# Score products of a differential-attention head in program order: the two maps take turns on the two halves of the TensorE array

## The chip, the cores and the metric

The kernel runs on one core of a Trainium2 chip. The metric is device time in microseconds (us) of one execution; lower is better.

## What is computed

The reference is one encoder block on 1024 tokens of width 1024, all in float32: an adaLN modulation, one input projection for two groups of heads, their attention, an output projection, a SwiGLU feed-forward part and a last RMSNorm. The change is in the products of queries and keys. Group A (8 heads of 64 channels) attends within a window of the grid; group B is differential attention, 4 heads with two softmax maps each:

```python
s = jnp.einsum('bhmqd,bhmkd->bhmqk', qb, kh).astype(jnp.float32)
s = s - slopes[:, None, None, None] * dist
p = jax.nn.softmax(s, axis=-1)
a = p[:, :, 0] - lam * p[:, :, 1]
return jnp.einsum('bhqk,bhke->bhqe', a.astype(vh.dtype), vh)
```

Here `m` counts the two maps of a head, each with 64 channels of its own for q and k.

## The kernel before

Every float32 product is made of three products of rounded parts: a value is split into a high part (type fp32r) and the rest, and high by high, low by high and high by low are summed in PSUM. So each score takes three matmuls.

The work runs in stages: modulation and the norm of x; the input projection and group A (class `Na`, PSUM tiles `ns`); group B (class `Da`, tiles `s`), which the trace shows from 305.7 to 607.2 us; the output projection; the feed-forward part (tiles `gu` and `dn`). Group B goes by units: one head h and 128 query rows i, 32 units in all. In this text unit "0_3" is head 0, i = 3.

A unit of group B does this:

- `Da.score` takes two PSUM tiles `s{h}_{i}_{m}` of 128x1024 from the pool `big`, which has two buffers; so map m of the next unit needs the buffer that map m of this one gives back. `scores` writes 12 matmuls for it, 6 for each map: two halves of 512 keys by three part products. Map 0 has its q and k in partitions 0 to 63, map 1 in 64 to 127 (`r = slice(64 * m, 64 * m + 64)`), and so each stands on its own half of the rows of the array. In the text of the program the maps alternate matmul by matmul.
- VectorE (DVE) reads each map out of PSUM (L686: adds the distances, takes the minimum), which frees the buffer; ScalarE (ACT) takes the exponent (L688).
- `Da.trans`: DVE combines the two maps (L701), TensorE transposes the result (tiles `at`), ACT copies it out of PSUM (`ath`, L708) and DVE makes the low part (`atl`, L709).
- `Da.pv`, after every second unit: 24 products with v (tiles `pv`).

Between these steps the list `seq` lets `fill` put in products of other stages as fillers: projections of the next heads (`q`, `k`, `v1p`), and for head 3 the output projection (`mo`). Their results leave the four PSUM buffers of the pool `bank` by ACT and DVE too (L460 and L461 for q, L468 and L469 for k). `next(mods)` puts in one step of the modulation on DVE (L602, `acc`).

What order an engine runs is set when the program is built: the tile framework schedules with its own timeline of costs, and keeps the order that it comes to. The class `InOrder` can hold instructions to the program's order by an edge (`after`) that costs no semaphore. On TensorE (`PE`) such edges are used for the first stage (`PE.chain`) and switched off before the heads; so in group B the scheduler chooses.

Of the kernel before, what the change touches and what calls it, by code (L numbers as in the profile page):

```python
# [104 lines left out]
def block_kernel(ctx: ExitStack, tc: tile.TileContext, t: dict):  # L105
    nc = tc.nc
    V, A, G, PE, SY = nc.vector, nc.scalar, nc.gpsimd, InOrder(tc, nc.tensor), nc.sync
# [74 lines left out]
    def rstd_of(ssq, name):  # L182
        r = sm.tile([P, 2], F32, tag="rstd", bufs=6, name=name)
        G.tensor_scalar(out=r[:, 0:1], in0=ssq, scalar1=1.0 / D, scalar2=EPS, op0=ALU.mult, op1=ALU.add)
        G.tensor_tensor(out=r[:, 1:2], in0=r[:, 0:1], in1=mhalf[:, 0:1], op=ALU.pow)
        return r[:, 1:2]
# [189 lines left out]
    for n in range(4):  # L376
        for j in range(4):
            PE.matmul(pms[0][:, 4 + n:5 + n], wada_t[0][j][:, n * P:(n + 1) * P], silc[:, j:j + 1],
                      start=j == 0, stop=j == 3)
# [263 lines left out]

    def scores(dsts, q, k, qsl, ksl):

        for ti, (z, w) in enumerate([(0, 0), (1, 0), (0, 1)]):
            for m in range(2):
                r = slice(64 * m, 64 * m + 64)
                PE.matmul(dsts[m], q[z][r, qsl], k[w][r, ksl], start=ti == 0, stop=ti == 2)

    def p_t(name):
        return mp.tile([P, S], F32, tag="p", bufs=4, name=name)
# [8 lines left out]
    class Da:  # L661
# [3 lines left out]
        def score(self):  # L665
            h, i = self.h, self.i
            if i == 0:
                need(("q", h)), need(("k", h))
                if h:
                    V.tensor_scalar(out=dists[0], in0=dists[0], scalar1=0.25, scalar2=None, op0=ALU.mult)  # L670
                else:
                    tp.close()
                    dp = mx.enter_context(tc.tile_pool(name="dp", bufs=1, reuse_waits="tile"))
                    dists.append(dp.tile([P, 1920], F16, name="dist"))
                    SY.dma_start(out=dists[0], in_=t["dist"])
            q, k = qkv["q", h], qkv["k", h]
            self.st = sm.tile([P, 8], F32, tag="st", bufs=12, name=f"st{h}_{i}")
            self.p = []
            ss = [big(f"s{h}_{i}_{m}") for m in range(2)]
            for n in range(2):  # L680
                nsl = slice(n * 512, (n + 1) * 512)
                scores([s[:, nsl] for s in ss], q, k, slice(i * P, (i + 1) * P), nsl)
            for m, s in enumerate(ss):
                pr = p_t(f"p{h}_{i}_{m}")
                d0 = (56 - 8 * i) * 16
                V.tensor_tensor_reduce(out=pr, in0=s, in1=dists[0][:, d0:d0 + 1024], scale=1.0, scalar=BIG,  # L686
                                       op0=ALU.add, op1=ALU.min, accum_out=self.st[:, m:m + 1])
                A.activation(out=pr, in_=pr, func=AF.Exp, scale=-1.0, bias=self.st[:, m:m + 1],  # L688
                             accum_out=self.st[:, 2 + m:3 + m])
                self.p.append(pr)  # L690
# [78 lines left out]
    class Na:  # L769
# [3 lines left out]
        def score(self):  # L773
            pr, i = self.pr, self.i
            if i == 0:
                need(("nq", pr)), need(("nk", pr)), tables(pr)
            q, k, tb = qkv["nq", pr], qkv["nk", pr], qkv["tb", pr]
            j0, j1 = max(i - 1, 0), min(i + 1, 7)
            self.nk, self.j0 = (j1 - j0 + 1) * P, j0
            nk = self.nk  # L780
            d0 = 384 if i == 0 else (640 if i == 7 else 0)
            s = big(f"ns{pr}_{i}")
            self.st = st = sm.tile([P, 8], F32, tag="st", bufs=12, name=f"nst{pr}_{i}")
            self.p = p = mp.tile([P, 2, 384], F32, tag="p", bufs=4, name=f"np{pr}_{i}")
            scores([s[:, m * 512:m * 512 + nk] for m in range(2)], q, k,
                   slice(i * P, (i + 1) * P), slice(j0 * P, j0 * P + nk))
            for m in range(2):
                V.tensor_tensor_reduce(out=p[:, m, 0:nk], in0=s[:, m * 512:m * 512 + nk],
                                       in1=tb[m][:, d0:d0 + nk], scale=1.0, scalar=BIG,
                                       op0=ALU.add, op1=ALU.min, accum_out=st[:, m:m + 1])  # L790
                A.activation(out=p[:, m, 0:nk], in_=p[:, m, 0:nk], func=AF.Exp, scale=-1.0,
                             bias=st[:, m:m + 1], accum_out=st[:, 2 + m:3 + m])
# [346 lines left out]
    for gi, fs in enumerate(groups):  # L1139
# [42 lines left out]
        for i in range(NT):  # L1182
            isl = slice((i % 4) * P, (i % 4 + 1) * P)
            last = gi == len(groups) - 1
# [14 lines left out]
            if last:  # L1199
                V.tensor_tensor(out=ssq[:, 0:1], in0=ssq[:, 0:1], in1=ssq[:, 1:2], op=ALU.add)  # L1200
                r = rstd_of(ssq[:, 0:1], f"r3_{i}")
# [55 lines left out]
```

## Time and profile before

| | |
|---|---|
| median of 3 runs | 1409.25 us (1408.97 to 1409.38) |
| the profiled execution | 1409.35 us |
| its span, first to last instruction | 1407.6 us |
| mean granted TensorE clock | 0.985 |
| TensorE (PE) busy | 1370.6 us, 97% |
| VectorE (DVE) busy | 719.6 us, 51% |
| ScalarE (ACT) busy | 461.0 us, 33% |

The time of the execution is 1.75 us more than its span. Matmuls are pipelined: a row of the timeline gives the start of the first one, the time from there to the end of the last, and how many were merged; the end of a matmul is modelled, and the next can start before it. So the pace of matmuls is read from starts, and a group's length from a merged row. `x12` in a row of tile `s` is 12 matmuls without another tile between them; both maps have the same name there, since buffer numbers are left out.

### The profile page before, as it was taken

Reading aid. Unit: us, or ns where it says so; the run is one execution under the profiler, and the core shown is the slowest. Engines: PE = TensorE matmul, PEld = TensorE weight load, DVE = VectorE, ACT = ScalarE, POOL = GpSimd, SP = SyncE. Lnnn points to the kernel's source line nnn. Section 1 sums busy time; section 2 is a strip of 40 time slices with the busy share of each in tenths; the row PEclk is TensorE's granted clock in tenths of the full one; section 3 lists DMA queues with packets and bytes.
Section 4 is the critical chain, followed back from the end, with each engine's and each line's share of the span. In section 5 each row is a group of like instructions: output and inputs, shape, how many; then the busy total and the mean of one; then the engine's idle time right before and its main releaser. Section 6 shows DMA issues by size and latency. Waiting matters only on the chain.

```text
span 1407.6 us, 17672 instructions
## 1 busy us (share of the span) xinstructions
PE 1370.6 (97%) x7033; PEld 1136.7 (81%) x7033; DVE 719.6 (51%) x1324; ACT 461.0 (33%) x817; POOL 290.3 (21%) x318
## 2 busy tenths in 40 slices
PE   6899999999999999999999999999999999999997
PEld 5698888887887778878888888888888888888886
DVE  5765678768767688757837125113411421251136
ACT  5554544545443454434521110211121021202212
POOL 3012332321121100002422221221221031204201
PEclk7999999999999999999999999999999999999999
DMA  9222523431221251022331120210111121103102
GB/s 370 111 75 78 170 91 117 173 127 45 68 84 59 91 202 38 8 84 97 120 105 35 56 60 7 84 60 30 56 55 40 31 75 45 60 1 90 45 27 93
DMA packets 43826, 114.82 MB, mean 82 GB/s; under 512 B 12723, under 2 KB 12979, under 8 KB 42464
## 3 DMA queue, kind: packets, MB, share of 16 engines
q1 hardware_dynamic: 39280, 99.37, 20.9%
q0 software_dynamic: 4464, 14.33, 3.2%
q8 instruction: 55, 0.90, 0.3%
q14 instruction: 27, 0.22, 0.0%
HBM read 99.26 MB, written 14.42 MB: 81 GB/s over the span
## 4 chain that ended last, share of the span: by engine, by line
PE 91%; DVE 3%; ACT 2%; DMA 2%; issue 1%; POOL 1%; SPq 0%; DVEq 0%; POOLq 0%; ACTq 0%
PE gu L89 33%; PE dn L89 17%; PE s L89 5%; PE pv L89 3%; PE mo L89 3%; PE q L89 3%; PE k L89 3%; PE nk L89 2%; PE mp L89 2%; PE npv L89 2%; PE at L89 2%; PE v1p L89 2%; PE v0p L89 2%; PE v3p L89 2%; PE v2p L89 2%; PE nq L89 2%
## 5 line engine op out<-in xcount | busy, mean ns | idle before, releaser
L1164 DVE TENSOR_TENSOR sg<-sg,gu 128x512 f32<-128x512 f32 x44 | 30.2, 687 | 352.6 <-ACT sg L1163 352.6
L89 PE MATMUL dn<-wd_h,al 128*128 128x512 f32 x352 | 136.9, 389 | 0.0
L89 PE MATMUL dn<-wd_l,ah 128*128 128x512 f32 x352 | 136.9, 389 | 0.0
L89 PE MATMUL dn<-wd_h,ah 128*128 128x512 f32 x352 | 136.9, 389 | 0.0
L1194 DVE TENSOR_TENSOR dt<-dn,gate_f 128x512 f32<-128x512 f32 x96 | 66.4, 691 | 88.1 <-PE dn L89 88.1
L202 POOL TENSOR_TENSOR wg_l<-wg_r,wg_h 128x1024 fp32r<-128x1024 f32 x20 | 48.3, 2417 | 271.9 <-ACT wg_h L201 271.9
L201 ACT ACTIVATE wg_h<-wg_r 128x1024 fp32r<-128x1024 f32 x22 | 23.3, 1060 | 211.9 <-PE dn L89 154.2
L688 ACT ACTIVATE p<-p,st 128x1024 f32<-128x1024 f32 x64 | 73.4, 1148 | 58.8 <-DVE st L686 57.9
L686 DVE CUSTOM_DVE_ANT_0 p<-s,dist 128x1024 f32<-128x1024 f32 x64 | 76.7, 1220 | 19.2 <-PE s L89 18.4
L89 PE MATMUL s<-qk 64*128 64x512 f32 x384 | 82.5, 415 | 1.5 <-DVE st L686 1.5
L202 POOL TENSOR_TENSOR wd_l<-wd_r,wd_h 128x1024 fp32r<-128x1024 f32 x20 | 48.0, 2399 | 163.7 <-ACT wd_h L201 163.7
L89 PEld LDWEIGHTS dn<-wd_h,al 128*128 128x128 f32 x352 | 66.1, 188 | 13.7
L89 PEld LDWEIGHTS dn<-wd_h,ah 128*128 128x128 f32 x352 | 66.1, 188 | 13.7
L89 PEld LDWEIGHTS dn<-wd_l,ah 128*128 128x128 f32 x352 | 66.1, 188 | 13.7
L1163 ACT ACTIVATE sg<-gu 128x512 f32<-128x512 f32 x44 | 26.0, 590 | 138.9 <-PE gu L89 136.6
L1195 DVE TENSOR_TENSOR x<-x,dt 128x512 f32<-128x512 f32 x96 | 70.0, 729 | 2.9
L89 PEld LDWEIGHTS s<-qk 64*128 64x128 f32 x384 | 50.9, 184 | 22.7 <-issue 8.1
L89 PE MATMUL gu<-h2h,wg_h 128*128 128x512 f32 x176 | 68.9, 392 | 0.2 <-DVE sg L1164 0.2
L591 POOL DMA_DIRECT2D wm<-in_w_ada_l_dram x48 | 27.4, 570 | 202.2 <-DVE acc L602 100.7
L89 PE MATMUL gu<-h2l,wg_h 128*128 128x512 f32 x176 | 68.7, 391 | 0.0
L89 PE MATMUL gu<-h2h,wu_h 128*128 128x512 f32 x176 | 68.6, 390 | 0.0
L89 PE MATMUL gu<-h2l,wu_h 128*128 128x512 f32 x176 | 68.6, 390 | 0.0
(308 smaller groups left out, 3500.1 us busy)
## 6 DMA issues: line engine op xcount, KB each, us to landing
w_r<-in_w_in_dram SPq DMA_DIRECT2D x24, 512.0 KB, 3.9
wm<-in_w_ada_l_dram POOLq DMA_DIRECT2D x48, 256.0 KB, 3.0
wg_r<-in_w_gate_up_dram SPq DMA_DIRECT2D x22, 512.0 KB, 3.5
wu_r<-in_w_gate_up_dram SPq DMA_DIRECT2D x22, 512.0 KB, 3.5
wd_r<-in_w_down_dram SPq DMA_DIRECT2D x22, 512.0 KB, 3.5
x<-in_x_dram SPq DMA_DIRECT2D x16, 512.0 KB, 8.5
wada<-in_w_ada_s_dram SPq DMA_DIRECT2D x6, 1024.0 KB, 12.1
v<-vd SPq DMA_DIRECT2D x4, 1024.0 KB, 5.7
```

The source lines that it names most:

```text
L89: ins = call(*args, **kw)
L201: A.activation(out=hi, in_=raw, func=AF.Copy)
L202: lo_engine().tensor_tensor(out=lo, in0=raw, in1=hi.bitcast(F32), op=ALU.subtract)
L591: queue.dma_start(out=raws[-1], in_=t["w_ada_l"][which - 2, n, :, j, :])
L686: V.tensor_tensor_reduce(out=pr, in0=s, in1=dists[0][:, d0:d0 + 1024], scale=1.0, scalar=BIG, op0=ALU.add, op1=ALU.min, accum_out=self.st[ ...
L688: A.activation(out=pr, in_=pr, func=AF.Exp, scale=-1.0, bias=self.st[:, m:m + 1], accum_out=self.st[:, 2 + m:3 + m])
L1163: A.activation(out=sg, in_=gu[:, 0:512], func=AF.Silu)
L1164: V.tensor_tensor(out=sg, in0=sg, in1=gu[:, 512:1024], op=ALU.mult)
L1194: V.tensor_tensor(out=dt_, in0=out, in1=gtf[:, dsl], op=ALU.mult)
L1195: V.tensor_tensor(out=x1[i][:, dsl], in0=x1[i][:, dsl], in1=dt_, op=ALU.add)
```

## The change

Each matmul of a call of `scores` gets an edge to the one before it, so that the alternation of the maps that the program's text has is kept. Nothing is added to or left out of what is computed, and the number of TensorE instructions in the program is the same.

```diff
     def scores(dsts, q, k, qsl, ksl):
 
+        last = None
         for ti, (z, w) in enumerate([(0, 0), (1, 0), (0, 1)]):
             for m in range(2):
                 r = slice(64 * m, 64 * m + 64)
-                PE.matmul(dsts[m], q[z][r, qsl], k[w][r, ksl], start=ti == 0, stop=ti == 2)
+                mm = PE.matmul(dsts[m], q[z][r, qsl], k[w][r, ksl], start=ti == 0, stop=ti == 2)
+                if last is not None:
+                    PE.after(mm, last)
+                last = mm
```

The TensorE order is the same up to unit 0_0; group A's scores alternate in both kernels. In group B, before, most units have all of map 0 and then all of map 1. TensorE at unit 0_1, before (`q1` is a projection for head 1, the names end in numbers of the buffers):

```order
L89 MATMUL q1_0_3262<-hh3_165,w16_l_3257 128x512
L89 MATMUL s0_1_0_3303<-qk0_2951 128x512 x6
L89 MATMUL s0_1_1_3304<-qk0_2951 128x512 x6
L89 MATMUL at0_0_0_3367<-ident_79,p0_0_0_3287 128x128 x4
L89 MATMUL at0_0_1_3374<-ident_79,p0_0_0_3287 128x128 x4
```

The same place now; of the 12 rows of the unit the last four stand here:

```order
L89 MATMUL s0_1_0_3303<-qk0_2951 128x512
L89 MATMUL s0_1_1_3304<-qk0_2951 128x512
L89 MATMUL s0_1_0_3303<-qk0_2951 128x512
L89 MATMUL s0_1_1_3304<-qk0_2951 128x512
L89 MATMUL at0_0_0_3367<-ident_79,p0_0_0_3287 128x128 x4
L89 MATMUL at0_0_1_3374<-ident_79,p0_0_0_3287 128x128 x4
```

Where six of one map stood ahead of six of the other, the maps now alternate to the end. The transposes of unit 0_0 follow at once in both orders.

TensorE at unit 0_3, before:

```order
L89 MATMUL at0_1_0_3426<-ident_79,p0_1_0_3317 128x128 x4
L89 MATMUL at0_1_1_3433<-ident_79,p0_1_0_3317 128x128 x4
L89 MATMUL s0_3_0_3447<-qk0_2951 128x512 x6
L89 MATMUL s0_3_1_3448<-qk0_2951 128x512 x6
L89 MATMUL pv0_0_3473<-ath0_0_0_3360,v0_0_3344 128x256
L89 MATMUL s0_4_0_3540<-qk0_2951 128x512 x6
L89 MATMUL pv0_0_3473<-atl0_0_0_3362,v0_0_3344 128x256
```

And now:

```order
L89 MATMUL at0_1_0_3426<-ident_79,p0_1_0_3317 128x128 x4
L89 MATMUL at0_1_1_3433<-ident_79,p0_1_0_3317 128x128 x4
L89 MATMUL s0_3_0_3447<-qk0_2951 128x512
L89 MATMUL pv0_0_3473<-ath0_0_0_3360,v0_0_3344 128x256
L89 MATMUL s0_3_1_3448<-qk0_2951 128x512
L89 MATMUL s0_3_0_3447<-qk0_2951 128x512
L89 MATMUL s0_3_1_3448<-qk0_2951 128x512
```

One matmul of map 0 now stands alone, with one filler behind it, and then the other 11; map 0 can no longer be finished before map 1's buffer is free. Map 0 of unit 0_4 has left this place: it came one matmul behind unit 0_3, and now it comes after all 24 products `pv0_0`, the transposes of unit 0_2 and nine products of a projection.

DVE around the read of unit 1_7, before (L461 takes the low part of the projection `q2` out of PSUM, ISA at L686 is the read of a map):

```order
L701 SCALAR_TENSOR_TENSOR p1_6_0_4505<-p1_6_1_4508,st1_6_4490,p1_6_0_4505 128x1024
L709 TENSOR_TENSOR atl1_2_1_4463<-at1_4_1_4474,ath1_2_1_4461 128x4x128
L602 SCALAR_TENSOR_TENSOR acc41_4132<-wm414_4263,silc_89,acc41_4132 128x512
L686 ISA p1_7_0_4593,st1_7_4578<-s1_7_0_4579,dist_3270 128x1024
L686 ISA st1_7_4578 128x1
L461 SCALAR_TENSOR_TENSOR qk2_4353<-q2_1_4453,qk2_4353 128x512
```

And now (the lines have moved by four):

```order
L461 SCALAR_TENSOR_TENSOR qk2_4353<-q2_1_4453,qk2_4353 128x512
L702 RECIPROCAL st1_6_4490<-st1_6_4490 128x1
L703 SCALAR_TENSOR_TENSOR st1_6_4490<-st1_6_4490,lam_620 128x1
L705 SCALAR_TENSOR_TENSOR p1_6_0_4505<-p1_6_1_4508,st1_6_4490,p1_6_0_4505 128x1024
L713 TENSOR_TENSOR atl1_2_0_4462<-at1_5_0_4544,ath1_2_0_4460 128x4x128
L690 ISA p1_7_0_4593,st1_7_4578<-s1_7_0_4579,dist_3270 128x1024
```

The read of `q2_1` was behind the combination of unit 1_6 and the first read of unit 1_7, and is now ahead of both. On TensorE the products `k2_0` followed unit 1_7's scores by 12 small products; now those small products come ahead of the scores, and `k2_0` right behind.

## Rows read from the trace of the kernel before

**Rows 1.** The page, parts 1 and 4: busy time of each engine, and the chain by engine.
```profile
PE 1370.6 (97%) x7033; PEld 1136.7 (81%) x7033; DVE 719.6 (51%) x1324; ACT 461.0 (33%) x817; POOL 290.3 (21%) x318
...
PE 91%; DVE 3%; ACT 2%; DMA 2%; issue 1%; POOL 1%; SPq 0%; DVEq 0%; POOLq 0%; ACTq 0%
```

**Rows 2.** Windows of head 0 and group B: busy PE, PEld, DVE, ACT, POOL, clock, DMA.
```profile
305.70:362.80 57.10, 56.72 (x299) 43.02 (x298) 44.01 (x89) 28.26 (x51) 7.05 (x11) 1.00 0.20 70
...
305.70:607.20 301.50, 297.24 (x1705) 236.82 (x1705) 223.40 (x418) 139.83 (x236) 31.03 (x32) 0.98 0.22 77
```

**Rows 3.** The page, part 5, group B's scores: busy us, mean ns, idle before.
```profile
L89 PE MATMUL s<-qk 64*128 64x512 f32 x384 | 82.5, 415 | 1.5 <-DVE st L686 1.5
...
L89 PEld LDWEIGHTS s<-qk 64*128 64x128 f32 x384 | 50.9, 184 | 22.7 <-issue 8.1
```

**Rows 4.** Timeline of PE: start us, length us, engine, line, tiles, count.
```profile
312.52 2.24 PE L89 MATMUL s<-qk 64*128 64x512 f32 x12
...
335.01 0.40 PE L89 MATMUL k<-hh,w_h 128*128 128x512 f32 x1
...
335.24 0.39 PE L89 MATMUL k<-hl,w_h 128*128 128x512 f32 x1
...
368.68 0.50 PE L89 MATMUL s<-qk 64*128 64x512 f32 x1
...
377.06 1.65 PE L89 MATMUL s<-qk 64*128 64x512 f32 x6
...
389.89 0.28 PE L89 MATMUL v1p<-w_h,hl 128*128 128x256 f32 x1
390.01 0.28 PE L89 MATMUL v1p<-w_l,hh 128*128 128x256 f32 x1
390.22 1.65 PE L89 MATMUL s<-qk 64*128 64x512 f32 x12
```

**Rows 5.** Timeline of all engines, from unit 0_0's first read to its transposes.
```profile
308.54 1.23 DVE L686 CUSTOM_DVE_ANT_0 p<-s,dist 128x1024 f32<-128x1024 f32 x1 [4.22 <-PE s L89]
...
313.24 1.29 DVE L701 SCALAR_TENSOR_TENSOR p<-p,st,p 128x1024 f32<-128x1024 f32 x1
...
314.69 1.09 PE L89 MATMUL at<-ident,p 128*128 128x128 f32 x8
```

**Rows 6.** Timeline of DVE: the two reads of unit 1_2.
```profile
391.91 1.23 DVE L686 CUSTOM_DVE_ANT_0 p<-s,dist 128x1024 f32<-128x1024 f32 x1 [1.18 <-PE s L89]
...
393.06 1.22 DVE L686 CUSTOM_DVE_ANT_0 p<-s,dist 128x1024 f32<-128x1024 f32 x1
```

**Rows 7.** Groups of DVE in 305.7 to 607.2: busy, mean ns, idle before and releasers.
```profile
L686 DVE CUSTOM_DVE_ANT_0 p<-s,dist 128x1024 f32<-128x1024 f32 x62 | 74.4, 1220 | 19.1 <-PE s L89 18.4 <-PE at L89 0.4
L709 DVE TENSOR_TENSOR atl<-at,ath 128x512 fp32r<-128x512 f32 x60 | 40.3, 685 | 23.0 <-ACT ath L708 23.0
```

**Rows 8.** Timeline at 441 us: DVE's read of q2_1, and PE behind it.
```profile
440.99 0.68 DVE L461 SCALAR_TENSOR_TENSOR qk<-q,qk 128x512 fp32r<-128x512 f32 x1
...
441.72 0.79 PE L89 MATMUL k<-hh,w_h 128*128 128x512 f32 x1 [2.31 <-DVE qk L461]
442.31 0.63 PE L89 MATMUL k<-hl,w_h 128*128 128x512 f32 x1
442.74 0.63 PE L89 MATMUL k<-hh,w_l 128*128 128x512 f32 x1
```

**Rows 9.** Windows with a low clock (columns as in rows 2, the clock behind POOL).
```profile
441.00:448.00 7.00, 6.28 (x15) 4.94 (x16) 6.96 (x18) 2.48 (x4) 1.04 (x1) 0.51 0.25 99
...
516.00:519.60 3.60, 3.60 (x16) 3.23 (x15) 3.60 (x9) 1.99 (x5) 0.00 (x0) 0.53 1.03 421
```

**Rows 10.** Timeline at units 2_5 and 2_6: the last scores, the first read, the next scores.
```profile
508.23 1.43 PE L89 MATMUL s<-qk 64*128 64x512 f32 x10
...
513.30 1.22 DVE L686 CUSTOM_DVE_ANT_0 p<-s,dist 128x1024 f32<-128x1024 f32 x1
...
514.59 1.67 PE L89 MATMUL s<-qk 64*128 64x512 f32 x6 [1.08 <-DVE st L686]
```

## The prediction

> **What bounds the kernel now.** I read the busy time by engine first. TensorE is busy 97% of the span and is 91% of the chain that ended last [rows 1], so a TensorE stretch that gets shorter shortens the kernel, as long as nobody else is late. Then I cut out group B, the only place where the order changes. In its 301.5 us TensorE is busy 297.2 and VectorE 223.4; in head 0, which has the fewest fillers, VectorE is busy 44.0 of 57.1 us, 77% [rows 2]. So the stage is TensorE's, with VectorE a quarter behind.
>
> Next comes what the scores take there. Their 384 matmuls have TensorE busy for 82.5 us, with only 1.5 us of idle time before them [rows 3]. The timeline then says what an order is worth [rows 4]. At 377.06 six matmuls of one map take 1.65 us. At 390.22 twelve matmuls, which happen to alternate there, also take 1.65 us. At 312.52 twelve that go six by six take 2.24 us. So two matmuls on the two halves of the array run in the time of one, and before the change this happens in few places: by the order, 66 of the 192 matmuls of map 1 stand right behind one of map 0. In the changed order it is 178.
>
> **The change part by part.** *Scores.* Counted in the order of the changed kernel, they stand in 54 pieces. 23 are long: 16 with all 12 matmuls alternating, and 7 with 11, the first of map 0 having gone ahead; at 1.65 us [rows 4] they make 38.0. Ten are a single matmul of map 0; one takes 0.50 us [rows 4], together 5.0. The other 21 pieces hold 57 steps of a pair (or one left over). A further pair costs (1.65 - 0.50) / 5 = 0.23 us, which is also the distance of two full 512-column matmuls, 335.01 to 335.24 [rows 4]. So they take 21 x 0.50 + 36 x 0.23 = 18.8. The sum is 61.8 against 82.5 [rows 3]: **-20.7 us**.
>
> One mechanism could spoil that step: a half's next weights might have to wait until its matmul is done. A load of weights takes 184 ns [rows 3], so a step would be 0.184 + 0.23 = 0.41 us, where the row at 390.22 shows 0.23 for each pair. The Trainium skill, "TensorE: Matmul & The Clock Gate", Part 3, says that a weight load overlaps matmuls in flight only when its row group differs, which would make that wait the rule for alternating pairs too. By it the sum would be 23 x (0.50 + 5 x 0.41) + 5.0 + 21 x 0.50 + 36 x 0.41 = 89.0, so 6.5 us more than now. The measured row disagrees with it, and the sum goes by the row.
>
> *The edges* cost nothing by themselves: they order instructions of one engine and no semaphore is added.
>
> *New waits.* Until now map 0 of the next unit could start when map 0 of this unit had been read. Now the twelve are tied together, so they need both buffers. Both maps also finish together; the two reads then end at 393.06 + 1.22 = 394.28, 2.4 us after the scores that ended at 390.22 + 1.65 [rows 4, 6]. Where TensorE has less than that to do in between, it stands still, and the fillers, transposes and products with v behind it in its queue with it. I priced what stands between two units in the changed order by rows 4 (0.23 for 512 columns, 0.12 for 256, as 389.89 to 390.01) and row 314.69 for eight transposes [rows 5]. Of 31 gaps three are below 2.4: units 0_2 to 0_3 (1.5 us with the lone matmul: wait 0.9), 2_3 to 2_4 (1.5: 1.0) and 0_4 to 0_5 (2.3: 0.1). From 0_5 to 0_6 there are 2.9 us, but VectorE does two `atl` of 0.69 us [rows 7] and two like them between the pairs of reads; I take 1.3. After unit 0_0 the transposes wait for L701. That ends at 314.53 and they start at 314.69, just in time [rows 5]; as TensorE gets there 0.59 (2.24 - 1.65) and two 0.12 fillers earlier, it waits 0.8. At unit 2_6 VectorE is late: unit 2_5's scores end at 509.66, its first read starts at 513.30, and TensorE waits 1.08 for it [rows 10]. For the second read it would wait 1.2 to 1.7 longer if VectorE stays that late, and not at all if not: 0.8. The sum is **+4.9**, between 1.9 (the three gaps alone) and twice that.
>
> *Waits that go.* At 441.72 the projection `k2_0` waits 2.31 us for VectorE's L461, which starts at 440.99 [rows 8]. In the new order L461 is ahead of a combination of 1.29 us [rows 5] and a read of 1.22, and `k2_0` comes a piece of 1.65 us later: the wait goes. With it goes the low clock behind it. TensorE is at 0.51 of its clock (its level of 1.2 GHz) for 7.0 us [rows 9], matmuls start 0.43 apart instead of 0.23 [rows 4, 8], and half of the 7 us is lost. Unit 0_4's wait, 1.5 - 1.08 = 0.4 [rows 3, 10], goes too, since its scores have moved behind 24 products. **-2.3 - 3.4 - 0.4 = -6.1**; nothing at worst, if another collision comes in their place.
>
> *Clock.* A new wait can lower the clock again. Behind the waits at 510 to 516 it was at 0.53 for 3.6 us [rows 9], which loses 1.7. I take one such stretch, **+1.7**, with 0 and four of them, 6.8, as ends.
>
> *Other queues.* POOL has the memset that opens head 2's q buffer behind one more weight split, SP has a weight load and an x load on the other side of a neighbour. Each is needed only after tens of products of other tiles, which hide it; without that cover the memset would cost a split, some 2.4 us.
>
> The terms make -20.7 + 4.9 - 6.1 + 1.7 = -20.2. VectorE sets a limit a little below that. It idles 18.4 us waiting for scores [rows 7], and 223.4 us of work and its other waits, above all 23.0 for ScalarE [rows 7], stay, so the stage can hardly shrink by more than 18.4. I take **-18.4**. The profiled execution took 1409.35 us, 0.1 more than the median of the runs, so the forecast is **1391.0 us**; by itself it may be 1386 to 1396.
>
> **The rivals.** *VectorE takes half of it back.* With alternating maps its first read cannot start before nearly all twelve matmuls are done, whereas it used to read map 0 while TensorE made map 1. If only half of the 18.4 us goes, the time is 1400.1. For it: 77% busy in head 0, which would be 83% with the 20.7 us spread evenly over group B. Against it: the waits shown lie where TensorE has most fillers, so VectorE has time. The Trainium skill, "TensorEngine Tiling (Array Packing)", section PSUM Bottleneck, warns that packing speeds up TensorE but not the evacuation of PSUM, which may become the bottleneck; no row shows that yet. Chance 0.20.
>
> *All waits vanish*: no new ones, the old ones gone, -26.8: 1382.6. Against it are the three gaps below 2.4. Chance 0.10.
>
> *Slower.* At unit 1_2, where both maps already finish together, VectorE waits 1.18 us for them [rows 6]. If each of 32 units cost it that and it had no slack, 37.8 us would stand in place of 18.4: the stage would be 19.4 longer, 1428.8. It decides from 18.4 / 32 = 0.58 us for each unit on. Against it: that wait stands in a stretch full of `v1p` products, where VectorE had run out of work and TensorE never waited for it. Chance 0.03. The weight-load mechanism above, 1409.35 + 6.5 = 1415.9, has the direct row against it: 0.01.
>
> *It does nothing*: the pairs save what is lost at waits nobody saw, or the scheduler's fillers would have hidden it: 1409. Against it is TensorE's 99% in group B [rows 2], where there is nothing to hide behind. Chance 0.04.
>
> **How the numbers follow.** The forecast has the remaining 0.62. The range, 1385 to 1402, reaches from near the second rival, over the forecast's own range, past the first. A measurement can tell about 0.2%, 2.8 us, from no change. Faster by more than that are the forecast and the first two rivals, 0.92; within it the last, 0.04; slower the others, 0.04.
>
> **What would show it.** Right: the group of score matmuls near 62 us busy instead of 82.5; rows of 12 at 1.65 us and none at 2.24; group B near 283 us; the 2.31 wait of `k2_0` gone; TensorE waits of about 1 us before units 0_3, 0_6 and 2_4; VectorE waiting less for scores. Wrong: rows of 12 alternating that take over 2 us (the pairs don't overlap); score busy time at 62 but idle time before scores and transposes above 10 us (VectorE is the bound); more stretches at half clock than now.

## The result and the profile after

The changed kernel takes **1392.63 us** (median of four runs, 1391.39 to 1393.89), against 1409.11 us (1407.70 to 1409.38) for the kernel before on the same chip: ratio 0.9885, 95% interval 0.9868 to 0.9902. The forecast was 1391.0, with a range of 1385 to 1402. The profiled execution took 1391.83 us, 17.5 less than the one before; its span is 1390.0.

The page's busy time by engine (answers to [rows 1]):

```profile
PE 1347.5 (97%) x7033; PEld 1118.0 (80%) x7033; DVE 721.2 (52%) x1324; ACT 460.6 (33%) x817; POOL 289.5 (21%) x318
```

TensorE lost 23.1 us of busy time over the whole span, with the same 7033 records. The other engines do what they did. The span fell by 17.6 only, so 5.5 us came back as idle time: 3.4 of them in group B, and most of the rest ahead of 300 us, where both kernels run the same order.

The windows of group B after (columns as in [rows 2]), and of a stretch with a low clock in it (answers to [rows 9]):

```profile
305.70:590.20 284.50, 276.84 (x1712) 220.71 (x1710) 225.32 (x418) 139.62 (x236) 30.58 (x32) 0.99 0.23 81
...
485.10:488.50 3.40, 3.40 (x16) 2.47 (x13) 3.37 (x9) 0.92 (x2) 0.00 (x0) 0.50 0.20 77
```

Group B takes 284.5 us instead of 301.5, 17.0 of the 17.6. TensorE was idle in it for 4.3 us, now for 7.7. The two stretches at half clock in it (6.8 and 3.4 us) have become one of 3.4, at 0.50, TensorE's level of 1.2 GHz; just ahead of it TensorE had twice waited at unit 2_4.

The scores' matmuls and weight loads by group (answers to [rows 3]):

```profile
L89 PE MATMUL s<-qk 64*128 64x512 f32 x384 | 64.6, 424 | 3.4 <-DVE st L690 3.4
...
L89 PEld LDWEIGHTS s<-qk 64*128 64x128 f32 x384 | 36.6, 187 | 22.3 <-issue 8.1 <-DVE st L690 5.3 <-DVE atl L713 1.4
```

One matmul still takes what it took (424 ns against 415), but the 384 together are busy for 64.6 us instead of 82.5: more of them lie beside each other. The weight loads shrink in the same way, from 50.9 to 36.6, at 187 ns each. The matmuls' idle time before them, all of it for VectorE's reads, has grown from 1.5 to 3.4.

The timeline of TensorE at units 0_1 and 2_4 and at the projection `k2` (answers to [rows 4, 5, 8]):

```profile
312.31 1.65 PE L89 MATMUL s<-qk 64*128 64x512 f32 x12
314.51 0.66 PE L89 MATMUL at<-ident,p 128*128 128x128 f32 x4 [0.55 <-DVE p L705]
...
444.54 0.50 PE L89 MATMUL k<-hh,w_h 128*128 128x512 f32 x1 [1.03 <-DVE o L769]
...
483.60 0.49 PE L89 MATMUL s<-qk 64*128 64x512 f32 x1 [0.49 <-DVE st L690]
484.74 2.67 PE L89 MATMUL s<-qk 64*128 64x512 f32 x11 [0.65 <-DVE st L690]
```

Unit 0_1's row of twelve, 2.24 us before, now takes 1.65. Right behind it stands the forecast wait for the combination. The 2.31 us wait ahead of `k2_0` has gone, and 1.03 has come up one product tile later, at `k2_1`, behind another VectorE instruction. Unit 2_4 shows what a late read now does: its first matmul waits for one buffer, runs alone, and the other 11 wait for the second. They then take 2.67 us instead of 1.65, since the clock is at 0.50 from 485.1 on.

TensorE's waits from 300 to 660 us, the five largest (the last columns are total, times, longest):

```profile
PE s L89 <- DVE st L690: 3.4, 6, 0.9
PE bc L89 <- DVE rda L753: 1.7, 1, 1.7
PE k L89 <- DVE o L769: 1.0, 1, 1.0
PE bc L89 <- DVE qk L469: 1.0, 1, 1.0
PE at L89 <- DVE qk L469: 0.8, 2, 0.6
```

All are for VectorE, but none is longer than 1.7, and that one (at 612.9, behind group B) was there before. VectorE's own idle time in group B, by group (answers to [rows 7]):

```profile
L690 DVE CUSTOM_DVE_ANT_0 p<-s,dist 128x1024 f32<-128x1024 f32 x62 | 73.5, 1217 | 8.6 <-PE s L89 8.5
L713 DVE TENSOR_TENSOR atl<-at,ath 128x512 fp32r<-128x512 f32 x60 | 39.9, 684 | 17.7 <-ACT ath L712 17.7
```

VectorE waits 8.5 us for scores instead of 18.4, and 17.7 for `ath` instead of 23.0. So it was not moved to the limit: it still idles 284.5 - 225.3 = 59.2 us of the stage.

### The profile page after: what moved, and what is told of

It is laid out like the page before. It is cut to its first block, busy times and chain, and to the rows that moved or that the text cites. A ratio compares the mean times of both kernels' runs of the same rounds, so it can differ in the third digit from the quotient of the medians.

```text
span 1390.0 us, 17663 instructions
## 1 busy us (share of the span) xinstructions
PE 1347.5 (97%) x7033; PEld 1118.0 (80%) x7033; DVE 721.2 (52%) x1324; ACT 460.6 (33%) x817; POOL 289.5 (21%) x318
## 4 chain that ended last, share of the span: by engine, by line
PE 62%; DVE 3%; DMA 1%; issue 1%; ACT 0%; POOL 0%; SPq 0%; DVEq 0%; POOLq 0%; ACTq 0%
PE gu L89 33%; PE dn L89 17%; PE mo L89 3%; PE mp L89 2%; PE pv L89 2%; PE s L89 2%; PE at L89 1%; PE mpb L89 1%; PE q L89 1%; DVE p L690 1%; PE k L89 1%; DMA wo_0r<-in_w_out_dram 0%; DVE n2v L1111 0%; DMA wm<-in_w_ada_l_dram 0%; DMA ol<-o_dram 0%
## 5 line engine op out<-in xcount | busy, mean ns | idle before, releaser
L89 PE MATMUL gu<-h2h,wu_l 128*128 128x512 f32 x176 | 68.5, 389 | 0.0
L89 PE MATMUL gu<-h2h,wg_l 128*128 128x512 f32 x176 | 68.5, 389 | 0.0
```

The source lines that it names most:

```text
L89: ins = call(*args, **kw)
```

## The experiments

The theory: what the change gains is the overlap of the two halves of the array, and what it costs is that a unit's twelve matmuls now need both buffers at once. The rivals are that the gain comes from the new places of the fillers, and that VectorE sets the new time.

### The same ties, without the pairs

The twelve score matmuls of a unit in group B are tied in one row, but in the order 000000111111 (the digit is the map):

```diff
...
+    def block_scores(ss, q, k, qsl):
+
+        last = None
+        for m in range(2):
+            r = slice(64 * m, 64 * m + 64)
+            for n in range(2):
+                nsl = slice(n * 512, (n + 1) * 512)
+                for ti, (z, w) in enumerate([(0, 0), (1, 0), (0, 1)]):
+                    mm = PE.matmul(ss[m][:, nsl], q[z][r, qsl], k[w][r, nsl], start=ti == 0, stop=ti == 2)
+                    if last is not None:
+                        PE.after(mm, last)
+                    last = mm
...
-            for n in range(2):
-                nsl = slice(n * 512, (n + 1) * 512)
-                scores([s[:, nsl] for s in ss], q, k, slice(i * P, (i + 1) * P), nsl)
+            block_scores(ss, q, k, slice(i * P, (i + 1) * P))
```

> Group B's twelve score matmuls of a unit tied in the other order: six of map 0, then six of map 1, over both halves of the keys. Theory (TensorE sets the pace, and the gain is the overlap of the two halves): the busy time of the scores goes back to 83 us or more, a unit in one piece takes 2.24 us instead of 1.65, and the kernel takes 1406 to 1415 us. Rival (the gain came from the new places of fillers, which a tie brings in any order): 1398 us or less.

Measured: 1408.81 us (1407.77 to 1411.43) against 1408.82 before, ratio 1.0005 (0.9994 to 1.0015). Its scores and its window of group B:

```profile
L89 PE MATMUL s<-qk 64*128 64x512 f32 x384 | 88.8, 413 | 0.0
```

```profile
305.70:607.00 301.30, 300.27 (x1715) 240.16 (x1714) 223.82 (x419) 139.99 (x236) 32.69 (x32) 1.00 0.22 77
```

The scores are 6.3 us longer than before the change; what TensorE no longer idles (1.0 against 4.3) and the clock that no longer falls pay for that. So the ties gain nothing by themselves. What the new places of the fillers are worth this run cannot show: by the two orders, only 10 of the 1281 other TensorE instructions between group B's first and last score have moved past twelve or more score matmuls, a unit's worth, from where they stood before the change; in the changed kernel 150 have. That rival is answered by the account below, where the scores' own busy time falls by 17.9 us and the span by 17.6.

### The ties in heads 0 and 1 only

```diff
...
-    def scores(dsts, q, k, qsl, ksl):
+    def scores(dsts, q, k, qsl, ksl, tied=True):
...
-                if last is not None:
+                if tied and last is not None:
...
-                scores([s[:, nsl] for s in ss], q, k, slice(i * P, (i + 1) * P), nsl)
+                scores([s[:, nsl] for s in ss], q, k, slice(i * P, (i + 1) * P), nsl, tied=h < 2)
```

> The ties only in heads 0 and 1 of group B; heads 2 and 3 as before the change. Theory: the gain adds up head by head with the pairs, and heads 0 and 1 gave 10 to 11 us of it by the two traces (the last product k2_1 comes 10.6 us earlier): 1398 to 1400 us. Rival (most of the gain is one wait, that of k2_0, and the clock behind it, with the rest lost to new waits): 1402 us or more if heads 2 and 3 gave the rest, 1395 or less if they gave nothing.

Measured: 1398.66 us (1396.69 to 1399.49), ratio 0.9930 (0.9914 to 0.9946), scores 75.2 us busy. The scores' gain goes with the tied heads, as it should if it is a sum over units. It is not the whole of this run's gain: of the 10.3 us by which its span is shorter, 7.3 are scores. Half clock gives 5.1, and idle time and the rest take 0.9 and 1.2 (the account below). So this run alone does not rule out that the wait of `k2_0` and the clock behind it, which lie at the end of head 1, are a good part of what heads 0 and 1 gain.

### Group A without alternation

Group A's scores alternate in both kernels. Here they are written in blocks of three, 000111 instead of 010101; group B is as after the change:

```diff
...
-    def scores(dsts, q, k, qsl, ksl):
+    def scores(dsts, q, k, qsl, ksl, block=False):
...
-        for ti, (z, w) in enumerate([(0, 0), (1, 0), (0, 1)]):
-            for m in range(2):
+        parts = [(0, 0), (1, 0), (0, 1)]
+        for ti, m in [(ti, m) for m in range(2) for ti in range(3)] if block else [(ti, m) for ti in range(3) for m in range(2)]:
+                z, w = parts[ti]
...
-                   slice(i * P, (i + 1) * P), slice(j0 * P, j0 * P + nk))
+                   slice(i * P, (i + 1) * P), slice(j0 * P, j0 * P + nk), block=True)
```

> Group B as changed; in group A the six score matmuls of a unit, which alternated before and after the change, go three of map 0 and then three of map 1. Theory: a piece takes five steps of a pair instead of three, about 0.35 us more for 384 columns and 0.24 for 256, so 24 x 0.35 + 8 x 0.24 = 10 us more score time, and since TensorE is busy nearly all of that stage, 1400 to 1404 us. Rival (the pairs' time is hidden beside VectorE): under 2 us more, 1391 to 1395.

Measured: 1391.51 us (1390.41 to 1393.80), ratio 0.9884 (0.9867 to 0.9900). This is a miss: nothing was lost. The timeline of TensorE, a row of six of group A's scores, first in this kernel, then in the changed kernel:

```profile
97.89 0.80 PE L89 MATMUL ns<-qk 64*128 64x384 f32 x6
```

```profile
97.14 0.79 PE L89 MATMUL ns<-qk 64*128 64x384 f32 x6
```

Blocks of three take 0.80 us where alternating matmuls take 0.79, and all 144 matmuls of this shape are busy for 19.6 us against 19.1, where the theory's 24 x 0.35 made 8.4 more. So two neighbours on different halves are not what it needs. Looking back at [rows 4], the row 000000111111 of the kernel before says the same: at 2.24 it is well below the 3.30 of two rows of six. So the theory had to be put wider: each half seems to take its next matmul from some places ahead in TensorE's queue, past matmuls of the other half that wait for theirs.

### Blocks of three in group B

The first experiment again, with the loops over `m` and `n` exchanged: 000111000111.

> The twelve score matmuls of a unit of group B in one tied row, as in the run with the maps in blocks of six (1408.81 us, scores 88.8 us busy), but in blocks of three: 000111000111. Theory formed after the run with group A in blocks of three (each half of the array takes its next matmul from a few places ahead in the queue, so three of one map may stand between two of the other): a whole row of twelve takes 1.65 to 1.75 us, the scores are 70 to 75 us busy (the rows that are cut by fillers between the maps don't pair), and the time is 1391 to 1397. Rival, my theory until then (only neighbours of different maps overlap): a row of twelve has 9 steps and takes 0.50 + 8 x 0.23 = 2.34 us, scores 81 to 86 busy, time 1402 to 1408.

Measured: 1397.86 us (1395.04 to 1400.50) against 1410.70 on that chip, ratio 0.9914 (0.9890 to 0.9938). Scores by group and a row of twelve in the timeline:

```profile
L89 PE MATMUL s<-qk 64*128 64x512 f32 x384 | 72.5, 418 | 1.7 <-DVE st L701 1.7
```

```profile
313.35 1.66 PE L89 MATMUL s<-qk 64*128 64x512 f32 x12
```

Row and busy time are those of the wider theory; the time lies 0.9 above its upper end, with two stretches at half clock in group B (3.4 us each). The scheduler cuts this kernel's scores and those of the first experiment into as many pieces, 59, so their difference, 88.8 against 72.5 us busy, lies in the order inside the pieces. From the traces of these two and of the kernel before, the lengths of pieces by their pattern (0 and 1 may change places):

| matmuls in the piece | length in us | steps of 0.23 behind the first 0.50 |
|---|---|---|
| 000 | 0.94 to 0.97 | 2 |
| 010101, or 000111 | 0.96 to 0.97 | 2 |
| 000000 | 1.65 to 1.67 | 5 |
| 00000011 | 1.65 to 1.66 | 5 |
| 010101010101, or 000111000111 (9 of 11; the others 1.99 and 2.17) | 1.65 to 1.67 | 5 |
| 000000111111 | 2.22 to 2.25 | 7.5 |
| 0 alone | 0.49 to 0.50 | 0 |

A block of two or three of the other map is free; two blocks of six, without overlap 11 steps, save 3.5 of them. A piece costs what its longer map costs, as long as the other map's turn comes within three or four matmuls. What is still lost here against the alternation (72.5 against 64.6) are mostly the pieces that fillers cut inside a block or between two blocks, twelve of them a bare 000.

### Pairs with room between the units

Behind a unit's scores in the program's text:

```diff
                 scores([s[:, nsl] for s in ss], q, k, slice(i * P, (i + 1) * P), nsl)
+            PE.floor, PE.left = PE.last, 12
```

With it the 12 TensorE instructions that the program writes next get an edge behind the unit's last score. The scheduler can no longer pull them ahead of the unit or between its matmuls, so they stay as room behind it; by the order, lone matmuls fall from ten to two.

> As changed, and in group B the next twelve TensorE instructions that the program makes after a unit's scores are held behind them. By the order this leaves 2 lone matmuls instead of 10 and 47 pieces instead of 54, price 58.0 us instead of 61.8, and the gaps between units 0_2 and 0_3, 2_3 and 2_4, 2_5 and 2_6 grow from 0.9, 1.5 and 2.4 us of other work to 4.1, 5.8 and 3.7. Theory (lone matmuls and the waits for both buffers cost what is still lost): 1383 to 1388 us, with waits before scores under 1 us. Rival (VectorE already sets the pace of group B, so waits only move): 1390 to 1394 us.

Measured: **1383.30 us** (1382.49 to 1384.30), ratio 0.9823 (0.9808 to 0.9838), so it is faster than both kernels. Scores, the window of group B, VectorE's groups there, and TensorE's two largest waits from 300 to 581 us:

```profile
L89 PE MATMUL s<-qk 64*128 64x512 f32 x384 | 60.5, 418 | 2.8 <-DVE st L691 1.8 <-ACT qk L468 0.8 <-DVE ptl L823 0.2
```

```profile
305.70:581.00 275.30, 270.61 (x1709) 219.50 (x1709) 224.99 (x418) 138.52 (x236) 31.24 (x32) 1.00 0.25 84
```

```profile
L691 DVE CUSTOM_DVE_ANT_0 p<-s,dist 128x1024 f32<-128x1024 f32 x62 | 73.3, 1220 | 4.0 <-PE s L89 3.9
L714 DVE TENSOR_TENSOR atl<-at,ath 128x512 fp32r<-128x512 f32 x60 | 40.1, 685 | 11.8 <-ACT ath L713 11.7
```

```profile
PE s L89 <- DVE st L691: 1.8, 4, 0.7
PE k L89 <- DVE o L770: 1.0, 1, 1.0
```

The time is the theory's. The waits before scores are 2.8 us in all, 1.8 of them for reads; its "under 1 us" holds for each of them and not for their sum. Against the change alone the waits for reads halve, the scores get shorter by another 4.1 us, and group B has no stretch at half clock. VectorE is busy 225.0 of 275.3 us and is still no bound. So the rival with VectorE falls.

### Room between the units, without the ties

The kernel before, with that one line alone.

> The kernel before (score matmuls not tied), with only this added: behind the scores of a unit the planner puts at least 12 instructions that are not in order of need before the next unit's may stand. Theory (the pairs are the gain, the spacing only lets the tied rows stand whole and takes waits away): most rows stay in mixed order, scores 73 to 78 us busy instead of 82.5, and the time is 1397 to 1403, well above the 1383.3 of pairs and spacing together. Rival (the spacing is what gains in that version, whatever the order of the maps): 1383 to 1392.

(The words "instructions that are not in order of need" there mean the 12 that the program writes next.) Measured: 1395.50 us (1393.25 to 1396.15), ratio 0.9894 (0.9869 to 0.9919): below the theory's range and above the rival's, so a miss, though a partial one. Its scores:

```profile
L89 PE MATMUL s<-qk 64*128 64x512 f32 x384 | 72.9, 416 | 0.6 <-ACT qk L468 0.3 <-DVE st L687 0.2
```

The expectation for the scores was 73 to 78. The one line cuts fewer pieces (50 instead of 58) and leaves more rows mixed, so it gains on pairs too, 9.6 us of scores. Of half clock, which the expectation left out, it has 3.4 us in group B instead of 10.2. Of the ten rows 000000111111 that it still has nine take 2.21 to 2.24 us. The room and the ties thus overlap in what they gain: 15.2 us (room) and 16.5 us (ties) apart, 25.5 together.

### Fewer cuts still

The version with pairs and room, with the first score of each half tied behind the instruction that came last in the program:

```diff
-        last = None
+        last = PE.last
```

> Pairs and spacing as in the version of 1383.3 us, and the first score matmul of a unit's half tied behind the instruction that the planner put last, so that fewer rows are cut: by the order 26 whole rows of 12 instead of 19, and 2 lone matmuls. Theory (time follows the scores' busy time, as long as VectorE has over 3 us from one unit to the next): scores 57 to 59 us busy instead of 60.5, time 1379 to 1383. Rival (fillers that can no longer go between the halves make TensorE wait for VectorE elsewhere): no better than 1383, with more than 4 us of waits for scores and transposes.

Measured: 1398.18 us (1396.50 to 1399.15), ratio 0.9915 (0.9895 to 0.9936): a miss, and what the rival said. Its scores, and TensorE's largest waits from 300 to 660 us:

```profile
L89 PE MATMUL s<-qk 64*128 64x512 f32 x384 | 57.8, 414 | 0.8 <-DVE st L691 0.6 <-DVE ptl L823 0.2
```

```profile
PE at L89 <- DVE p L706: 2.3, 1, 2.3
PE pv L89 <- ACT ath L713: 2.2, 1, 2.2
PE mo L89 <- DVE x L986: 1.9, 1, 1.9
PE at L89 <- DVE o L770: 1.7, 1, 1.7
```

The scores are the shortest of all and hardly wait, just as meant. But TensorE now idles 14.2 us in group B, mostly before transposes, products with v and projections, and three stretches fall to half clock. By the orders, some scores now stand behind instructions that they stood ahead of, as the new edge asks: unit 1_7's, for one, behind 12 products of `k2`. That such moves bring these waits is likely, but no run shows it. The fewest cuts are not the best order.

### The account

For each profiled execution: the scores' busy time, TensorE's idle time from 300.0 us to the end of group B (800.4 us before the end of the span, as 607.2 is in the kernel before), and half of the length of the stretches at half clock there. The last column is the span less these three.

| kernel | span | scores | idle | half clock | rest |
|---|---|---|---|---|---|
| before | 1407.6 | 82.5 | 4.3 | 5.1 | 1315.7 |
| after | 1390.0 | 64.6 | 7.7 | 1.7 | 1316.0 |
| blocks of six | 1406.8 | 88.8 | 1.0 | 0 | 1317.0 |
| heads 0 and 1 | 1397.3 | 75.2 | 5.2 | 0 | 1316.9 |
| group A in threes | 1388.7 | 63.6 | 7.8 | 0 | 1317.3 |
| blocks of three | 1396.6 | 72.5 | 3.1 | 3.4 | 1317.6 |
| room alone | 1393.6 | 72.9 | 3.5 | 1.7 | 1315.5 |
| pairs and room | 1380.8 | 60.5 | 4.9 | 0 | 1315.4 |
| fewer cuts | 1396.9 | 57.8 | 14.2 | 5.1 | 1319.8 |

The rest stays within 2.2 us in the first eight. It holds what half clock costs outside group B: the ninth has a stretch of 3.4 us at 160 us, worth up to 1.7, and behind group B the changed kernel, heads 0 and 1 and blocks of three have 6.8 us of it where the others have 3.4. A score at half clock counts in two columns, in the changed kernel for 1.0 us. Three numbers thus account for spans that differ by 26 us.

## Why the prediction was right, and where its steps were not

**Scores.** The mechanism and its price hold: of the 16 whole rows of twelve 12 take 1.65 or 1.66, the seven of 11 take 1.65 to 1.67, the ten lone matmuls 0.49 or 0.50. The step said 61.8 us, measured are 64.6: the gain is 17.9 and not 20.7. The term was short by 2.8: by what late buffers do to a row, and by the clock. A late buffer breaks the row: the lone first matmul costs 0.49 us of busy time on top of the 1.65 of the other 11. That happened at units 0_6, 2_4 and 2_6, 1.5 us. At half clock unit 2_4's row took 1.0 longer. Unit 1_5's row took 0.3 longer without a gap, also behind a late read (VectorE, then TensorE):

```profile
408.59 1.22 DVE L690 CUSTOM_DVE_ANT_0 p<-s,dist 128x1024 f32<-128x1024 f32 x1
...
409.57 1.94 PE L89 MATMUL s<-qk 64*128 64x512 f32 x12
```

The second read of unit 1_4 ends at 409.81; the row's second matmul, which follows the first at once in the other rows, starts at 409.87. I had priced the waits, and not what they do to a row.

**The weight loads.** The rival that a half's next weights wait until its matmul is done would have made 89.0 us of scores; 64.6 is the answer. The Trainium skill, "TensorE: Matmul & The Clock Gate", Part 3, adds that matmuls start and end in the order of the program; the rows of 000111 in the time of 000 (0.97 against 0.96) don't go with that either, and the measured rows decide.

**New waits.** Of the six forecast places five came about: 0_2 to 0_3 with 1.0 us (said 0.9), 2_3 to 2_4 with 1.1 (1.0), `at0_0` 0.55 (0.8), 2_6 0.94 (0.8), and 0_5 to 0_6 0.33 (1.3); the sixth (0.1) didn't. Together 4.0 against 4.9. But places that I had not looked at add 1.0 before `k2_1`, 1.0 before a `bc` at 359.7, 0.6 and 0.4 around unit 2_4's transposes, and some of 0.2. By the account the idle time grew by 3.4, where the step had 4.9 - 2.3 - 0.4 = 2.2. (Its lower end, 1.9, should be 2.0 by its own three waits.)

**Waits that go, and the clock.** `k2_0`'s 2.31 us and the 7 us of low clock behind it are gone, as forecast; that another collision comes in their place was the bound I named, and at `k2_1` a smaller one did. Of half clock I had 1.7 us less in all; it is 3.4 less, since the stretch at 516 went too, and one of 3.4 us came, at unit 2_4.

**The sum.** -17.9 + 3.4 - 3.4 = -17.9, against -17.6 in span; the terms of the text made -20.2. What the scores' term lacked (2.8) and the idle time (1.2) was partly made up by the clock, which gave 1.7 more than forecast.

**The cut from 20.2 to 18.4** brought the number closer, for a wrong reason. It said that the stage could hardly shrink by more than VectorE's 18.4 us of waiting for scores. The version with pairs and room shrinks the stage by 301.5 - 275.3 = 26.2 us, and VectorE still waits 3.9 for scores: its other idle time shrinks as well, the one for `ath` from 23.0 to 11.7. Idle time of an engine that isn't the bound is no budget. Less than 20.2 came by the scores' broken and late rows and the waits nobody had looked at.

**Rivals.** *VectorE takes half back* (1400.1) did not come. The Trainium skill, "TensorEngine Tiling (Array Packing)", section PSUM Bottleneck, is borne out in kind and not in size: TensorE's waits for the reads of PSUM rose from 1.5 to 3.4 us. *All waits vanish* (1382.6) is not this kernel; the version with room came to 1383.3, by shorter scores and with 4.9 us of idle time left. *It does nothing* (1409) is 16 us off. *Slower* would have needed 0.58 us of lost slack for each unit; VectorE instead waits 10 us less for scores. That the alternation is not needed inside three matmuls is something no step of the prediction used: its pricing by steps of a pair held because the changed order alternates throughout.

## What to carry to other kernels

Where two small matmuls can share the array, count from the order how many pieces there are and how long the longer half of each is; here that priced 384 matmuls within 5%. Blocks of three in one row were as good as strict alternation, blocks of six weren't. Before tying instructions that need several buffers, write down what stands between one group and the next: each late buffer costs its wait and a broken row, and a few other instructions held behind the group can be worth as much as the ties themselves.

## What the runs showed of the hardware that was not expected

TensorE does not need neighbours on different halves of the array to run them together. Two blocks of three, 000111, take 0.96 to 0.97 us, as long as one block; two blocks of six take 2.24 and not 1.65. The starts of the single matmuls in the traces say how far ahead a half gets. In 000111 they come in pairs, at 0, 0.01, 0.34, 0.34, 0.57 and 0.58 us. In the row 000000111111 at 312.52 of the kernel before they come at 0, 0.34, 0.57, 0.58, 0.80, 0.92 and so on, and the one at 0.58 lasts 0.49 us, as otherwise only the first of a half does (the rest last 0.38 to 0.39). So map 1 seems to begin with the third matmul of map 0, some four places before its turn, and from there takes its usual 1.65: 0.58 + 1.65 = 2.23. How a half passes the other no trace shows.

The clock doesn't fall to its lower level after every wait. The kernel with group A in threes idles 7.8 us in group B and has none; blocks of three idles 3.1 and has two. Which waits bring it on stays open; no run here isolates it.
